# Recurrence bounds in the first three steps, and the output gate's SiLU as one pass of ScalarE, in a hybrid attention and recurrence block

## The chip, the cores and the metric

The kernel runs on one core of a Trainium2 chip. The core has five engines, each with its own instruction queue that runs in order: TensorE (PE, matrix products into PSUM banks), VectorE (DVE), ScalarE (ACT, which applies functions from a loaded table), GpSimd (POOL) and SyncE (SP). SP, ACT and POOL can issue DMA transfers; in this kernel SP issues nearly all of them. The engines meet only through semaphores. The metric is the device time of one execution in microseconds (us); the median of several runs is compared.

## The reference

One layer of a trunk with 256 tokens and a width of 2048, in float32. The parts that matter here:

```python
a = rmsnorm(h, norm_mix_pre[layer])
proj = a @ w_in[layer]
q_a, k_a, v_a, q_r, f_r, i_r, g_r, gate_a, gate_r = split_columns(proj)
...
lower_bounds = jnp.cumsum(jax.nn.softmax(hgrn_lower_bounds, axis=0), axis=0)
lb = lower_bounds[layer].reshape(HGRN_HEADS, HGRN_KEY_DIM)[None, :, None, :]
q_h = jax.nn.silu(rheads(q_r))
f = lb + (1.0 - lb) * jax.nn.sigmoid(rheads(f_r))
r_out = hgrn2_chunked(q_h, jnp.log(f), 1.0 - f, rheads(i_r))
...
r_out = r_out * lax.rsqrt(jnp.mean(r_out * r_out, axis=-1, keepdims=True) + NORM_EPS)
r_out = r_out * hgrn_norm_gain[layer]
r_out = r_out.reshape(B, S, HGRN_HEADS * HGRN_VAL_DIM) * jax.nn.silu(g_r)
y = jax.nn.sigmoid(gate_a) * (attn @ w_attn_branch) + jax.nn.sigmoid(gate_r) * (r_out @ w_hgrn_branch)
h = h + rmsnorm(y @ w_mix_out, norm_mix_post)
```

A SwiGLU feed-forward layer with its own norms follows. The change touches two small things: how the 1024 lower bounds `lb` of the recurrence are made, and how the output gate, SiLU of `g_r` times the gain of the recurrence's norm, is made.

## The kernel before

**Products.** Every float32 weight tile is split into a high part (ACT rounds it) and a low part (DVE subtracts), and each product takes three matmuls: high by high, high by low, low by high. PE then runs an almost unbroken stream of matmuls. A *wide block* is 1024 columns of the projection, worked in 8 *steps* of 256 rows of depth. One step loads 1 MB of weights into one of three `raw` buffers (SP, lines 244 to 260), is split two steps ahead of its use (`split_wide`, line 333; a buffer is loaded again once its split is over), and is multiplied in `multiply_wide` (line 365).

**Plain steps and seven-product steps.** A plain step has 24 matmuls; its split is one pass of ACT (L342) and one of DVE (L344). For some pairs of rows a Strassen-like scheme with 21 matmuls is used: its split needs sums on DVE (L348, L354, L355), three passes of ACT (L353, L356, L359) and two more of DVE (L360 for `wl`, L362 for `dl`), and it uses sums of the activations, which `pair_sums` (line 449) makes once, for three pairs (0, 1 and 2), in four pieces each: f (L454), s (L434 to L438), a high part on ACT (L440) and a low part on DVE (L441).

**The first blocks.** Block 0 is the output gate `g_r` (steps 0 to 7, all plain). Block 1 is the first half of the branch gate `gate_a` (steps 8 to 15; steps 10, 12 and 14 have seven products), block 2 is its second half (steps 16 to 23; the same pattern), block 3 is the first half of `gate_r`. Block 0 adds into the four `acc` banks of PSUM; the others use `acc` and `aux` banks in turn.

**What sets the order.** The program order of each queue is fixed by the main loop (line 1394 on). In each step it first prepares (splits the tiles of two steps later, loads further ones), multiplies, advances the evacuations of finished blocks (`evacs`), and advances two *lanes*. A lane is a queue of generators, of which the first is advanced by one `yield`. In a wide block the lanes advance twice per step: once between the halves of the step's matmuls (line 286) and once at its end (line 1420). In block 0 the preparation, too, stands between the halves, behind the transposes of the next part of x (`more_x`, line 670).

Lane 0 holds `opening` (line 606) from the start:
- advances 1 to 8: squares of x on ACT (L596);
- advance 9 (middle of step 4): four DMAs on SP (gain row, feed-forward norm gain, lower bounds, rope table; L609 to L614), then the norm's factor `r1c` (`rsqrt_mean`, line 120: ACT Ln and Exp, a few tiny DVE operations) and the diagonal matrices for `row_broadcast` (line 542);
- advance 12: a matmul that spreads the factor; advance 13: ACT copies it to `rowb`;
- advance 14 (end of step 6): PE transposes 32 rows of `rowg` (L622);
- advance 15: DVE copies the columns to `colg` (L624), and takes maximum and differences (L627 to L629); ACT two Exp (L630, L631);
- advance 16: four tiny DVE operations give `lb` and `lb1` (L633 to L636);
- 24 empty advances, then at advances 40 to 43 the four rope tables on DVE (L641), and at 44 two mask loads on SP (L645, L646).

Lane 1 gets `pair_sums` in the middle of step 2 (advance 5), so its twelve pieces run at advances 5 to 16.

**The gate.** When step 7 is over, `evac_g` (line 749) takes block 0 out of the `acc` banks, two of its four keys at the end of step 7 and two at the end of step 8. Per key: ACT writes the sigmoid of the scaled bank into `sig` (L755), DVE multiplies the scaled bank with it (L756, which reads the bank a second time), and DVE multiplies with the gain row (L759). Block 1 needs the `acc` banks again from step 10 on. `stored` (line 728) evacuates blocks 1 to 3: DVE adds (L719), ACT's Sigmoid (L734), and a DMA from ACT's queue to memory (L737).

**Tables.** ACT's functions come from table sets, and the profile shows each exchange as an ACT_TABLE_LOAD on ACT. Line 152 asks for the set with Ln and Exp at the start. Elsewhere the program either asks ahead (`preload_act_table_set`), or a load is put directly ahead of the instruction that needs it when the kernel is built, as at L755.

Of the kernel before, what the change touches and what calls it, by code (L numbers as in the profile page):

```python
# [17 lines left out]
AF = mybir.ActivationFunctionType  # L18
OP = mybir.AluOpType

P = 128
# [59 lines left out]
def tile_hybrid_block(ctx: ExitStack, tc: tile.TileContext, t, out):  # L81
    nc = tc.nc
# [12 lines left out]
    def nm(s):  # L95
        serial[0] += 1
        return f"{s}_{serial[0]}"
# [7 lines left out]
    def aux():  # L105
        return auxp.tile([P, 512], F32, tag="aux", name=nm("aux"))
# [7 lines left out]
    def small(s, n=8, bufs=6):  # L114
        return cpool.tile([P, n], F32, tag=f"small{n}", bufs=bufs, name=nm(s))

    def mm(ps, lhsT, rhs, start, stop):
        nc.tensor.matmul(ps, lhsT, rhs, start=start, stop=stop, skip_group_check=True)  # L118

    def rsqrt_mean(dst, ss, n, bias=None):  # L120

        w = ss.shape[-1]
        v, y, a = (small(s)[:, :w] for s in ("v", "y", "a"))
        bias = bias or (eps[:, 0:1], eps[:, 1:2])
        nc.scalar.activation(y, ss, AF.Ln, scale=1.0 / n, bias=bias[0])
        nc.scalar.activation(y, y, AF.Exp, scale=-0.5)
        nc.vector.tensor_scalar(v, ss, -0.5 / n, bias[1], op0=OP.mult, op1=OP.add)  # L130
        if w == 1:
            nc.vector.scalar_tensor_tensor(out=a, in0=y, scalar=v, in1=y, op0=OP.mult, op1=OP.mult)
        else:
            nc.vector.tensor_mul(a, y, y)
            nc.vector.tensor_mul(a, a, v)
        nc.vector.scalar_tensor_tensor(
            out=dst, in0=a, scalar=1.5, in1=y, op0=OP.add, op1=OP.mult
        )
# [6 lines left out]
    ident = cpool.tile([P, P], F32, name="ident")  # L145
# [3 lines left out]
    nc.gpsimd.memset(eps[:, 1:2], -0.5 * EPS)  # L149
    rowg = cpool.tile([48, P], F32, name="rowg")  # L150
    nc.scalar.dma_start(rowg[0:16], t["norm_mix_pre"][0].rearrange("(a p) -> a p", p=P))
    nc.scalar.preload_act_table_set("natural_log_exp_and_others")
    colg = cpool.tile([P, 48], F32, name="colg")
    r1c = cpool.tile([P, 2], F32, name="r1c")
# [13 lines left out]
    lb = kp.tile([P, 120], F32, name="lb")[:, :8]  # L168
    lb1 = kp.tile([P, 8], F32, name="lb1")
# [4 lines left out]
    gainr = wide_pool[0].tile([P, HW], F32, name="gainr")  # L174
# [5 lines left out]
    def ptile(s):  # L180
        pool, n = (wide_pool[-1], 2) if wide_pool else (fp[0], 5)
        return pool.tile([P, 512], F32, tag="p", bufs=n, name=nm(s))
# [281 lines left out]
    class Split:  # L464
# [20 lines left out]
        def high(self, n, src):  # L485
            nc.scalar.activation(self.slots[n][:, :, 0, :], src, AF.Copy)

        def low(self, n, src):
            x = self.slots[n]
            nc.vector.tensor_sub(x[:, :, 1, :], src, x[:, :, 0, :].bitcast(F32))  # L490
            self.there.add(n)
# [22 lines left out]
    def transpose_in(src, gcol, dst, c, apart=False):  # L514

        ps = []
        for k in (2 * c, 2 * c + 1):
            if apart or not ps:
                bank = aux()
            ps.append(bank[:, :S] if apart else bank[:, (k % 2) * S : (k % 2 + 1) * S])  # L520
            for b in range(2):
                nc.tensor.transpose(  # L522
                    ps[-1][:, b * P : (b + 1) * P],
                    src[k // 4][:, b, (k % 4) * P : (k % 4 + 1) * P],
                    ident,
                )
        def high(kk):
            k = 2 * c + kk
            nc.scalar.activation(dst(k)[0], ps[kk], AF.Copy, scale=gcol[:, k : k + 1])  # L529

        def low(kk):
            k = 2 * c + kk
            nc.vector.scalar_tensor_tensor(
                out=dst(k)[1], in0=ps[kk], scalar=gcol[:, k : k + 1],
                in1=dst.f32(k), op0=OP.mult, op1=OP.subtract,
            )

        if apart:
            return high, low
        high(0), high(1), low(0), low(1)  # L540

    def row_broadcast(dst, rc):

        ds = [small("diag", P, 2) for _ in range(2)]
        for b in range(2):
            nc.vector.tensor_scalar(ds[b], ident, rc[:, b : b + 1], None, op0=OP.mult)
        yield
        yield
        yield
        ps = aux()  # L550
        for b in range(2):
            mm(ps[:, b * P : (b + 1) * P], ones[:, :P], ds[b], True, True)
        yield
        nc.scalar.activation(dst, ps[:, :S], AF.Copy)
# [4 lines left out]
    evacs, turns, lanes, queue = deque(), deque(), [deque(), deque()], deque()  # L559
    ready = set()  # L560
# [31 lines left out]
    def sumsq(dst, pieces):  # L592
        for j, x in enumerate(pieces):
            for b in range(2):
                junk = ptile("junk")
                nc.scalar.activation(  # L596
                    junk, x[:, b, :], AF.Square, accum_out=dst[:, 4 * b + j : 4 * b + j + 1]
                )
                yield

    def add_parts(dst, ss):
        nc.vector.tensor_reduce(
            dst, ss.rearrange("p (b j) -> p b j", b=2), op=OP.add, axis=mybir.AxisListType.X
        )

    def opening():
        ss, s2 = small("ss"), small("s2")
        yield from sumsq(ss, xt)
        nc.sync.dma_start(gainr, t["hgrn_norm_gain"].to_broadcast([P, HW]))  # L609
        nc.sync.dma_start(rowg[0:16], t["norm_ffn_pre"][0].rearrange("(a p) -> a p", p=P))  # L610
        nc.sync.dma_start(
            rowg[16:32], t["hgrn_lower_bounds"].rearrange("l (a p) -> (l a) p", p=P)
        )
        nc.sync.dma_start(cs, t["rope"])  # L614
        add_parts(s2[:, :2], ss)
        rsqrt_mean(r1c, s2[:, :2], D)
        ready.add("r1c")
        yield from row_broadcast(rowb, r1c)
        ready.add("rowb")
        yield  # L620
        ps = aux()
        nc.tensor.transpose(ps[:, :32], rowg[:32], ident[:32, :32])  # L622
        yield
        nc.vector.tensor_copy(colg[:, 16:48], ps[:, :32])  # L624
        l0, l1 = colg[:, 32:40], colg[:, 40:48]
        m, e0, e1 = small("m"), small("e0"), small("e1")
        nc.vector.tensor_max(m, l0, l1)  # L627
        nc.vector.tensor_sub(e0, l0, m)
        nc.vector.tensor_sub(e1, l1, m)  # L629
        nc.scalar.activation(e0, e0, AF.Exp)  # L630
        nc.scalar.activation(e1, e1, AF.Exp)  # L631
        yield
        nc.vector.tensor_add(e1, e0, e1)  # L633
        nc.vector.reciprocal(e1, e1)
        nc.vector.tensor_mul(lb, e0, e1)
        nc.vector.tensor_scalar(lb1, lb, -1.0, 1.0, op0=OP.mult, op1=OP.add)  # L636
        ready.add("lb")
        for _ in range(24):
            yield
        for i, (j, c) in enumerate(((0, -QSCALE), (1, -QSCALE), (0, 1.0), (1, 1.0))):  # L640
            nc.vector.scalar_tensor_tensor(  # L641
                out=tabs[:, i, :], in0=cs[:, j, :], scalar=c, in1=rowb, op0=OP.mult, op1=OP.mult
            )
            yield
        nc.sync.dma_start(amask, t["amask"])  # L645
        nc.sync.dma_start(lmask, t["lmask"])  # L646

    def keep_warm(n):

        ps = aux()  # L650
        for _ in range(n):
            mm(ps, warm[:, :P], warm, True, True)

    def start():
        keep_warm(WARM)
        ps = aux()
        nc.tensor.transpose(ps[:, :16], rowg[:16], ident[:16, :16])
        nc.vector.tensor_copy(colg[:, :16], ps[:, :16])
        high, low = transpose_in(xt, colg, xT, 0, True)
        for kk in range(2):  # L660
            high(kk)
            low(kk)
            split_first(0, kk)
        keep_warm(BRIDGE)
        transpose_in(xt, colg, xT, 1)
        split_first(0, 2)
        split_first(0, 3)
        lanes[0].append(opening())

    def more_x(c):  # L670
        if 0 < c < KD // 2 - 1:
# [5 lines left out]
    fT, qT, gN, iN = {}, {}, {}, {}  # L677
# [71 lines left out]
    def evac_g(b):  # L749
        def then(key, src):  # L750
            s, g = key
            if s == 0:
                gN[g] = hslot("g")
            sig = ptile("sig")
            nc.scalar.activation(sig, src, AF.Sigmoid, scale=r1c[:, s : s + 1])  # L755
            nc.vector.scalar_tensor_tensor(  # L756
                out=sig, in0=src, scalar=r1c[:, s : s + 1], in1=sig, op0=OP.mult, op1=OP.mult
            )
            nc.vector.tensor_mul(gN[g][:, s, :], sig, gainr[:, g * 512 : (g + 1) * 512])  # L759
        return totals(b, then)  # L760

    def nslot(s):
# [631 lines left out]
    for i in range(len(items)):  # L1394
        kind, n, _ = items[i]
# [92 lines left out]
```

## Time and profile before

| | |
|---|---|
| Median of three runs | 1722.13 us (1721.88 to 1722.79) |
| Profiled execution | 1722.56 us |
| Span of the profiled execution | 1720.8 us |
| Granted clock of TensorE | 0.998 |
| Steps 0 to 7 on PE (block 0) | 8.15 to 55.56 us |
| Steps 8 to 15 (block 1) | 55.56 to 102.61 us |
| DMA packets | 207189, 338.48 MB |

How to read what follows: a timeline row has the start in us, the duration (of all instructions merged into it), the engine (a "q" behind it is its queue's own work, as issuing a DMA), the source line, the operation, the tiles out<-in with their sizes, and the count. What stands in brackets is the idle time of the engine before it and what ended that: "[1.05 <-DVE dl L362]" means that the engine stood 1.05 us and went on when DVE had written `dl` in line 362. A group row has the line, engine, operation and tiles, the count, the durations (lowest, median and highest ns), and first and last start. A DMA row has the tiles, the queue, the count, the size and the median us from issue to landing. Matmul ends are modelled, since matmuls are pipelined; starts are the better measure, and a wait of PE seen by its starts is a little longer than the bracket says.

### The profile page before, as it was taken

Reading aid. Unit: us, or ns where it says so; the run is one execution under the profiler, and the core shown is the slowest. Engines: PE = TensorE matmul, PEld = TensorE weight load, DVE = VectorE, ACT = ScalarE, POOL = GpSimd, SP = SyncE. Lnnn points to the kernel's source line nnn. Section 1 sums busy time; section 2 is a strip of 40 time slices with the busy share of each in tenths; the row PEclk is TensorE's granted clock in tenths of the full one; section 3 lists DMA queues with packets and bytes.
Section 4 is the critical chain, followed back from the end, with each engine's and each line's share of the span. In section 5 each row is a group of like instructions: output and inputs, shape, how many; then the busy total and the mean of one; then the engine's idle time right before and its main releaser. Section 6 shows DMA issues by size and latency. Waiting matters only on the chain.

```text
span 1720.8 us, 21495 instructions
## 1 busy us (share of the span) xinstructions
PE 1703.5 (99%) x8356; PEld 1429.9 (83%) x8357; DVE 1358.7 (79%) x1486; ACT 898.7 (52%) x1016; POOL 6.5 (0%) x16
## 2 busy tenths in 40 slices
PE   9999999999999999999999999999999999999997
PEld 7788888888888888888888878888888888888886
DVE  6888888866787877774566578888888888898997
ACT  6455555544434434445444466555555555665663
POOL 0000000000000000000000000000000000000000
PEclk9999999999999999999999999999999999999999
DMA  8466666655544545475456745555556555656663
GB/s 289 162 237 241 232 221 220 229 189 194 172 159 160 197 135 163 155 254 187 159 172 204 245 163 196 196 197 200 201 202 202 201 202 197 221 191 215 201 197 114
DMA packets 207189, 338.48 MB, mean 197 GB/s; under 512 B 10688, under 2 KB 77424, under 8 KB 207088
## 3 DMA queue, kind: packets, MB, share of 16 engines
q1 hardware_dynamic: 201360, 325.71, 56.9%
q10 hardware_dynamic: 5728, 11.41, 1.8%
q8 instruction: 65, 1.06, 0.3%
q14 instruction: 36, 0.29, 0.1%
HBM read 328.69 MB, written 8.39 MB: 196 GB/s over the span
## 4 chain that ended last, share of the span: by engine, by line
PE 89%; DVE 6%; issue 2%; ACT 2%; DMA 1%; ACTq 0%; DVEq 0%; SPq 0%
PE acc L118 61%; PE aux L118 26%; DVE wl L344 1%; DVE wl L360 1%; DVE dl L362 1%; DVE sum L348 1%; ACT w L356 1%; ACT w L342 0%; PE aux L522 0%; DVE sum L355 0%; DVE sum L354 0%; PE aux L840 0%; DMA gpost<-in_norm_mix_post 0%; DMA raw<-in_w_ffn_gate_up 0%; PE aux L1166 0%
## 5 line engine op out<-in xcount | busy, mean ns | idle before, releaser
L297 DVE TENSOR_TENSOR w<-raw,w 128x1024 fp32r<-128x1024 f32 x224 | 274.1, 1224 | 194.9 <-ACT w L296 193.1
L296 ACT ACTIVATE w<-raw 128x1024 fp32r<-128x1024 f32 x224 | 237.0, 1058 | 292.8 <-PE acc L118 263.0
L118 PE MATMUL acc<-xT,w 128*128 128x256 f32 (+1 forms) x2048 | 366.6, 338 | 0.0
L118 PEld LDWEIGHTS acc<-xT,w 128*128 128x128 f32 x2048 | 311.6, 188 | 44.0
L344 DVE TENSOR_TENSOR wl<-raw,w 128x2048 fp32r<-128x2048 f32 (+1 forms) x131 | 284.1, 2173 | 48.7 <-ACT w L342 46.4
L342 ACT ACTIVATE w<-raw 128x2048 fp32r<-128x2048 f32 (+1 forms) x131 | 237.7, 1819 | 103.1 <-PE acc L118 34.9
L360 DVE TENSOR_TENSOR wl<-sum,w 128x2048 fp32r<-128x2048 f32 x63 | 144.3, 2291 | 57.4 <-ACT w L356 57.4
L118 PE MATMUL acc<-w,hT 128*128 128x512 f32 x622 | 183.1, 391 | 0.3 <-ACT hT L529 0.3
L118 PE MATMUL acc<-w,xT 128*128 128x512 f32 x578 | 169.4, 392 | 0.0
L353 ACT ACTIVATE w<-sum 128x1024 fp32r<-128x1024 f32 x63 | 67.0, 1063 | 195.6 <-DVE sum L348 195.6
L118 PE MATMUL aux<-w,hT 128*128 128x512 f32 x430 | 137.3, 389 | 0.0
L118 PEld LDWEIGHTS acc<-w,hT 128*128 128x128 f32 x622 | 116.1, 188 | 24.5 <-ACT hT L529 0.5
L118 PEld LDWEIGHTS acc<-w,xT 128*128 128x128 f32 x578 | 108.1, 188 | 22.2
L362 DVE TENSOR_TENSOR dl<-raw,dh 128x1536 fp32r<-128x1536 f32 x63 | 110.4, 1752 | 0.0
L118 PE MATMUL aux<-w,xT 128*128 128x512 f32 x344 | 109.8, 389 | 0.0
L359 ACT ACTIVATE dh<-raw 128x1536 fp32r<-128x1536 f32 x63 | 93.2, 1479 | 6.6 <-PE aux L118 3.4
L118 PEld LDWEIGHTS aux<-w,hT 128*128 128x128 f32 x430 | 80.7, 188 | 16.8
L118 PE MATMUL acc<-w,yT 128*128 128x512 f32 x384 | 88.2, 390 | 0.1
L118 PEld LDWEIGHTS acc<-w,yT 128*128 128x128 f32 x384 | 71.8, 188 | 15.3 <-DVE w L297 0.5
L118 PE MATMUL acc<-w,a 128*128 128x512 f32 x268 | 83.7, 389 | 0.5 <-DVE e L1200 0.5
L118 PE MATMUL aux<-w,a 128*128 128x512 f32 x268 | 83.7, 389 | 0.0
L118 PE MATMUL aux<-wl,hT 128*128 128x512 f32 x215 | 83.6, 389 | 0.0
(262 smaller groups left out, 2624.2 us busy)
## 6 DMA issues: line engine op xcount, KB each, us to landing
raw<-in_w_in SPq DMA_DIRECT2D x270, 512.0 KB, 4.6
raw<-in_w_ffn_gate_up SPq DMA_DIRECT2D x176, 512.0 KB, 4.6
raw<-in_w_ffn_down SPq DMA_DIRECT2D x88, 512.0 KB, 4.8
raw<-in_w_mix_out SPq DMA_DIRECT2D x32, 512.0 KB, 4.9
raw<-in_w_hgrn_branch SPq DMA_DIRECT2D x16, 512.0 KB, 4.6
raw<-in_w_attn_branch SPq DMA_DIRECT2D x16, 512.0 KB, 4.5
waits<-e ACTq DMA_DIRECT2D x24, 256.0 KB, 2.6
v<-waits SPq DMA_DIRECT2D x6, 512.0 KB, 7.0
```

The lines of the kernel that those rows point to most:

```text
L118: nc.tensor.matmul(ps, lhsT, rhs, start=start, stop=stop, skip_group_check=True)
L296: nc.scalar.activation(wh, raw, AF.Copy)
L297: nc.vector.tensor_sub(wl, raw, wh.bitcast(F32))
L342: nc.scalar.activation(hi[:, c], raw[:, c], AF.Copy)
L344: nc.vector.tensor_sub(lo[:, c], raw[:, c], hi[:, c].bitcast(F32))
L348: nc.vector.tensor_sub(s[:, :1024].rearrange("p (a c) -> p a c", a=2), raw[:, 512:1536].rearrange("p (a c) -> p a c", a=2), raw[:, None, : ...
L353: nc.scalar.activation(hi[:, :1024], s[:, :1024], AF.Copy)
L356: nc.scalar.activation(hi[:, 1024:], s[:, 1024:], AF.Copy)
L359: nc.scalar.activation(dhi, d, AF.Copy)
L360: nc.vector.tensor_sub(lo, s, hi.bitcast(F32))
L362: nc.vector.tensor_sub(dlo, d, dhi.bitcast(F32))
```

## The change

The two small loads of `rowg` (feed-forward norm gain and lower bounds) leave `opening`, where SP issued them at advance 9, and are issued by POOL at the start, into rows of their own. The bounds' transpose, copy and arithmetic become a generator of their own, `bounds`, which is put on lane 1 at the start: two empty advances, then its four pieces at advances 3 to 6. `pair_sums` comes into lane 1 behind it. `opening` loses three pieces' work and two of its advances, so the 24 empty advances, the rope tables and the mask loads come two advances earlier. Behind the norm's Ln and Exp, `opening` asks for the table set with Silu. `evac_g` writes Silu of the scaled bank straight into the gate's tile on ACT, and DVE does one product with the gain row.

```diff
@@ -149,6 +149,10 @@
     rowg = cpool.tile([48, P], F32, name="rowg")
     nc.scalar.dma_start(rowg[0:16], t["norm_mix_pre"][0].rearrange("(a p) -> a p", p=P))
+    nc.gpsimd.dma_start(rowg[16:32], t["norm_ffn_pre"][0].rearrange("(a p) -> a p", p=P))
+    nc.gpsimd.dma_start(
+        rowg[32:48], t["hgrn_lower_bounds"].rearrange("l (a p) -> (l a) p", p=P)
+    )
     nc.scalar.preload_act_table_set("natural_log_exp_and_others")
@@ -607,26 +611,38 @@
         nc.sync.dma_start(gainr, t["hgrn_norm_gain"].to_broadcast([P, HW]))
-        nc.sync.dma_start(rowg[0:16], t["norm_ffn_pre"][0].rearrange("(a p) -> a p", p=P))
-        nc.sync.dma_start(
-            rowg[16:32], t["hgrn_lower_bounds"].rearrange("l (a p) -> (l a) p", p=P)
-        )
         nc.sync.dma_start(cs, t["rope"])
         add_parts(s2[:, :2], ss)
         rsqrt_mean(r1c, s2[:, :2], D)
         ready.add("r1c")
+        nc.scalar.preload_act_table_set("silu_and_others")
         yield from row_broadcast(rowb, r1c)
         ready.add("rowb")
         yield
+        for _ in range(24):
+            yield
+        for i, (j, c) in enumerate(((0, -QSCALE), (1, -QSCALE), (0, 1.0), (1, 1.0))):
...
+        nc.sync.dma_start(amask, t["amask"])
+        nc.sync.dma_start(lmask, t["lmask"])
+
+    def bounds():
+
+        for _ in range(2):
+            yield
         ps = aux()
-        nc.tensor.transpose(ps[:, :32], rowg[:32], ident[:32, :32])
-        yield
-        nc.vector.tensor_copy(colg[:, 16:48], ps[:, :32])
+        nc.tensor.transpose(ps[:, :48], rowg, ident[:48, :48])
+        yield
+        nc.vector.tensor_copy(colg[:, 16:48], ps[:, 16:48])
...
         nc.vector.tensor_sub(e1, l1, m)
+        yield
         nc.scalar.activation(e0, e0, AF.Exp)
         nc.scalar.activation(e1, e1, AF.Exp)
         yield
@@ -635,15 +651,6 @@
         ready.add("lb")
-        for _ in range(24):
-            yield
-        for i, (j, c) in enumerate(((0, -QSCALE), (1, -QSCALE), (0, 1.0), (1, 1.0))):
...
-        nc.sync.dma_start(amask, t["amask"])
-        nc.sync.dma_start(lmask, t["lmask"])
@@ -666,6 +673,7 @@
         lanes[0].append(opening())
+        lanes[1].append(bounds())
@@ -751,12 +759,9 @@
-            sig = ptile("sig")
-            nc.scalar.activation(sig, src, AF.Sigmoid, scale=r1c[:, s : s + 1])
-            nc.vector.scalar_tensor_tensor(
-                out=sig, in0=src, scalar=r1c[:, s : s + 1], in1=sig, op0=OP.mult, op1=OP.mult
-            )
-            nc.vector.tensor_mul(gN[g][:, s, :], sig, gainr[:, g * 512 : (g + 1) * 512])
+            d = gN[g][:, s, :]
+            nc.scalar.activation(d, src, AF.Silu, scale=r1c[:, s : s + 1])
+            nc.vector.tensor_mul(d, d, gainr[:, g * 512 : (g + 1) * 512])
```

More of the change, by code (lines that the diff above doesn't have):

```diff
@@ L620, in opening @@
         yield
-        ps = aux()
-        nc.tensor.transpose(ps[:, :32], rowg[:32], ident[:32, :32])
-        yield
[L624 to L631, printed above, removed]
-        yield
[L633 to L637, printed above, removed]
         for _ in range(24):
@@ L646, in opening @@
         nc.sync.dma_start(lmask, t["lmask"])
+    def bounds():
+        for _ in range(2):
+            yield
+        ps = aux()
+        nc.tensor.transpose(ps[:, :48], rowg, ident[:48, :48])
+        yield
+        nc.vector.tensor_copy(colg[:, 16:48], ps[:, 16:48])
+        l0, l1 = colg[:, 32:40], colg[:, 40:48]
+        m, e0, e1 = small("m"), small("e0"), small("e1")
+        nc.vector.tensor_max(m, l0, l1)
+        nc.vector.tensor_sub(e0, l0, m)
+        nc.vector.tensor_sub(e1, l1, m)
+        yield
+        nc.scalar.activation(e0, e0, AF.Exp)
+        nc.scalar.activation(e1, e1, AF.Exp)
+        yield
+        nc.vector.tensor_add(e1, e0, e1)
+        nc.vector.reciprocal(e1, e1)
+        nc.vector.tensor_mul(lb, e0, e1)
+        nc.vector.tensor_scalar(lb1, lb, -1.0, 1.0, op0=OP.mult, op1=OP.add)
+        ready.add("lb")
     def keep_warm(n):
```

## The prediction

> **What bounds the kernel now.** I began with the page: which engine fills the span.
>
> ```profile
> span 1720.8 us, 21495 instructions
> PE 1703.5 (99%) x8356; PEld 1429.9 (83%) x8357; DVE 1358.7 (79%) x1486; ACT 898.7 (52%) x1016; POOL 6.5 (0%) x16
> ```
>
> PE is busy all but 17.3 us. The change adds and removes almost no PE work, so it can only win back time in which PE stands still, or lose more of it. Next came the stretches around the change, and who made PE wait over the whole run (in the windows: start:end, length, then busy time and instructions of PE, PEld, DVE, ACT and POOL, clock, DMA share, GB/s; in the waits: total, times, longest).
>
> ```profile
> 8.00:47.50 39.50, 39.50 (x191) 32.78 (x190) 28.81 (x48) 26.58 (x49) 0.00 (x0) 1.00 0.84 298
> 55.50:92.50 37.00, 32.91 (x141) 25.62 (x140) 31.69 (x36) 21.30 (x21) 0.00 (x0) 1.00 0.45 154
> ```
>
> ```profile
> PE acc L118 <- DVE wl L360: 1.7, 2, 1.5
> PE aux L118 <- DVE dl L362: 1.5, 2, 1.1
> ...
> PE acc L118 <- DVE sig L756: 0.9, 1, 0.9
> ```
>
> Up to 47.5 PE never rests. Between 55.5 and 92.5 it loses 4.1 of 37 us, with the clock at 1.00, waiting for VectorE (DVE): for the split weights (L360, L362), and once for the gate itself (L756). The PE timeline shows what the stretch would take without waits.
>
> ```profile
> 55.56 0.39 PE L118 MATMUL aux<-w,xT 128*128 128x512 f32 x1
> ...
> 85.62 0.39 PE L118 MATMUL aux<-w,xT 128*128 128x512 f32 x1
> ...
> 91.06 0.39 PE L118 MATMUL aux<-dh,xT 128*128 128x512 f32 x1
> 92.50 0.50 PE L118 MATMUL aux<-dl,xT 128*128 128x512 f32 x1 [1.05 <-DVE dl L362]
> ```
>
> The step from 85.62 to 91.06 has 24 matmuls, one every 0.227 us. Steps 8 to 13 have 24, 24, 21, 24, 21 and 24, and step 14 one before it needs dl: 139 in all, 31.5 us. So the matmul of 92.50 could start at 87.1. **At most 5.4 us are to be had.**
>
> **What DVE does in that stretch.** Its timeline decides how much of the 5.4 comes back.
>
> ```profile
> 52.02 0.68 DVE L454 TENSOR_TENSOR f<-xT 128x512 f32<-128x512 f32 x1
> ...
> 53.68 2.29 DVE L344 TENSOR_TENSOR wl<-raw,w 128x2048 fp32r<-128x2048 f32 x1
> 55.88 0.18 DVE L624 COPY colg<-aux 128x32 f32<-128x32 f32 x1
> ...
> 57.56 0.68 DVE L441 TENSOR_TENSOR so<-s,so 128x512 fp32r<-128x512 f32 x1
> 59.37 0.75 DVE L756 SCALAR_TENSOR_TENSOR sig<-acc,r1c,sig 128x512 f32<-128x512 f32 x1 [1.12 <-ACT sig L755]
> ...
> 61.54 0.69 DVE L759 TENSOR_TENSOR g<-sig,gainr 128x512 f32<-128x512 f32 x1
> 62.15 1.22 DVE L348 TENSOR_TENSOR sum<-raw 128x1024 f32<-128x1024 f32 x1
> ...
> 69.83 0.75 DVE L756 SCALAR_TENSOR_TENSOR sig<-acc,r1c,sig 128x512 f32<-128x512 f32 x1
> ...
> 72.61 2.28 DVE L344 TENSOR_TENSOR wl<-raw,w 128x2048 fp32r<-128x2048 f32 x1
> ...
> 90.69 1.75 DVE L362 TENSOR_TENSOR dl<-raw,dh 128x1536 fp32r<-128x1536 f32 x1
> ```
>
> ```profile
> 57.35 1.28 ACT L755 ACT_TABLE_LOAD   x1
> 58.64 1.27 ACT L755 ACTIVATE sig<-acc,r1c 128x512 f32<-128x512 f32 x2
> ```
>
> From 52.02 on DVE works or waits for ScalarE (ACT). From 55.88 to 57.56 stand the bounds; at 59.37 it waits 1.12 us for a sigmoid that stood behind a 1.28 us table load; then come two pairs of gate instructions, and only at 62.15 the sums that PE wants at step 10. The second two pairs run from 69.83 to 72.61. One DVE instruction starts about 0.08 before the last has ended (61.54 plus 0.69 is 62.23, the next starts at 62.15).
>
> **The new order, step by step.** Bounds leave this stretch. But they now lead lane 1 for six advances, so the pair sums behind them run two advances (one step) later. At 52.02 DVE now does the low part of pair 1 (0.68 less 0.08: 0.60) instead of f and s of pair 2 (53.68 less 52.02: 1.66); the split of step 9 runs from 52.62 to 54.82 (55.88 less 53.68: 2.20); f and s of pair 2 take until 56.48; two products (0.61 each) until 57.70. Silu delays none of this: its first two banks are full half way through step 7 (12 matmuls before 55.56: 52.8), ACT's copy for step 9 has to be over by 52.6 for DVE's split in any case, and its table is loaded. The sum L348 so starts at 57.70 instead of 62.15: **4.45 won.** From there to the next gate nothing changes (69.83 less 62.15: 7.68). Of the 2.78 us up to 72.61 there remain two products and the low part of pair 2: 1.82, **0.96 won.** Together 5.41; L362 ends 5.41 sooner and PE gets dl at 87.1, just as it arrives. Two limits nearly agree: 5.4.
>
> One activation each is a fair swap:
>
> ```profile
> 68.33 1.91 ACT L342 ACTIVATE w<-raw 128x2048 fp32r<-128x2048 f32 x1
> ```
>
> ```profile
> L1184 ACT ACTIVATE g<-acc,r2c x2: 679/684/688, 1036.0 to 1038.0; 128x512 f32<-128x512 f32 x2
> ```
>
> A Silu of this shape takes 684 ns; two sigmoids at 58.64 took 1.27. The accumulator banks are let go by ACT alone, before 64, so the wait on L756 goes. ACT's copy for step 11, at 68.33 before, moves up 4.45 with the sums and back 0.6 for pair 2's high part, now ahead of it: it ends at 66.4, and DVE wants it at 67.2, a margin of 0.8.
>
> **What moves into the opening.** I cost it at nothing: PE's transpose is moved, not added, and DVE is idle 10.7 of 39.5 us there. The cover is thinnest at step 5, where the Silu load now stands behind the norm, ahead of pair 0's high part and the activations of xT:
>
> ```profile
> 39.50 0.20 ACT L129 ACTIVATE y<-y 128x2 f32<-128x2 f32 x1
> ...
> 40.72 0.84 ACT L529 ACTIVATE xT<-aux,colg 128x256 fp32r<-128x256 f32 x2 [1.02 <-PE aux L522]
> ...
> 42.38 0.87 DVE L533 SCALAR_TENSOR_TENSOR xT<-aux,colg,xT 128x256 fp32r<-128x256 f32 x2
> ...
> 43.66 0.48 PE L118 MATMUL acc<-w,xT 128*128 128x512 f32 x1
> ```
>
> ACT has the norm's Exp done at 39.7; load and high part take it to 41.6, and xT's activations run 0.9 later. DVE, freed of f and s here, does one low part after 41.6 and L533 again at 42.3. Unchanged, with 0.4 us to spare (42.38 plus 0.87 is 43.25, due at 43.66).
>
> The two small loads leave SP's queue, behind which the rope and weight loads stand; those wait for DVE to free a buffer, so nothing is won. On POOL nothing is queued behind them until the recurrence. No POOL transfer is in this trace; the nearest rows:
>
> ```profile
> rowg<-in_norm_mix_pre ACTq DMA_DIRECT2D x1, 8.0 KB, 3.0
> ...
> rowg<-in_hgrn_lower_bounds SPq DMA_DIRECT2D x1, 8.0 KB, 5.8
> ```
>
> ```profile
> 16.42 0.60 PE L522 MATMUL aux<-ident,x 128*128 128x128 f32 x4
> ```
>
> From issue to landing they took 3.0 and 5.8. PE's FIFO reaches the moved transpose behind those of 16.42, at about 17 us: to be late the two would have to be issued at 11, and only a few memsets stand ahead of them on POOL. Nothing.
>
> **What the change gives back.** Block 1's gates still use Sigmoid (L734), and now Silu's table is the one loaded. Before, L755 had loaded Sigmoid's. No row shows Sigmoid behind Silu, so the price lies between 0 and one load, 1.28. I take the load, as one stood at 57.35 where Exp gave way to Sigmoid. It falls here, and the four rope tables (L641) come one step earlier:
>
> ```profile
> 109.46 0.71 ACT L734 ACTIVATE e<-e,r1c 128x512 f32<-128x512 f32 x1
> ...
> 113.75 2.29 DVE L344 TENSOR_TENSOR wl<-raw,w 128x2048 fp32r<-128x2048 f32 x1 [1.57 <-ACT w L342]
> ```
>
> ```profile
> 132.18 1.75 DVE L362 TENSOR_TENSOR dl<-raw,dh 128x1536 fp32r<-128x1536 f32 x1
> 133.85 0.76 DVE L641 SCALAR_TENSOR_TENSOR tabs<-cs,rowb 128x256 f32<-128x256 f32 x2
> ```
>
> ```profile
> 140.42 0.69 DVE L424 TENSOR_TENSOR e<-aux,e 128x512 f32<-128x512 f32 x1 [0.48 <-PE acc L118]
> ```
>
> ```profile
> 134.12 0.40 PE L118 MATMUL acc<-dl,xT 128*128 128x512 f32 x1
> ...
> 175.41 0.39 PE L118 MATMUL aux<-dh,xT 128*128 128x512 f32 x1
> ...
> 176.23 0.50 PE L118 MATMUL aux<-dl,xT 128*128 128x512 f32 x1 [0.43 <-DVE dl L362]
> ```
>
> Queued behind those sigmoids on ACT is the copy that DVE already awaits at 113.75, so DVE runs 1.28 plus 0.09 (a lost overlap) late. Two of the tables move from behind L362 to ahead of it: 0.76 less 0.08 more. At 132.18 DVE is 2.05 late, its dl ends at 133.93, and PE used it at 134.12 with 0.13 to spare: **PE loses 1.92.** At 176.23 PE waited 0.59 for the next dl (175.64 was its due time). DVE is only about 1 us late by then, because the tables are then done in both kernels and the wait of 0.48 at 140.42 shrinks; so those 0.59 come back: 1.33 lost. If the wait at 140.42 is truly PE's, it travels with PE, and 1.92 stays lost.
>
> The Trainium skill ("ScalarE: Activation LUTs", Table sets: the hidden batching unit) gives each set one expensive function and lists sigmoid as the anchor of a set of its own, and advises batching calls by set. That speaks against this change; by it the load at L734 is certain, without it the sum would be the first rival's. No run here shows it yet.
>
> **Sum.** 5.4 less 1.33 is 4.1, less 1.92 is 3.5; I take 3.9, nearer the first. The profiled execution took 1722.56 (1.8 around its span), 0.43 above the median of the three runs, and would go to 1718.7; from the median of 1722.13 it is **1718.2**.
>
> **Rivals.** (1) Silu's set holds Sigmoid, no second load: only the tables' 0.68 less 0.13 is lost: 5.4 less 0.55, 1717.3. (2) The exchange costs two loads' time, 2.56: DVE 3.3 late, PE loses 3.2 and gets 0.59 back, 2.8 won, 1719.3. For it: nothing in the rows, a sigmoid starts 0.01 behind the load at 57.35. The same page (What ACT_TABLE_LOAD costs) adds a drain of about 1.38 us to the 1.28, 2.66 together, nearly this case; the row at 58.64 shows no such gap behind the load. (3) Another order on ACT eats the win: in the opening the whole load, 1.28 less 0.4, reaches PE, or the 0.8 margin at step 11 fails by as much; 0.9 to 2 us less, 1719.1 to 1720.2. (4) The change does not do what it says: the bounds' time (55.88 to 57.56) and the wait at 59.37 don't come back, because the later pair sums and Silu's own wait fill them: 5.4 less 2.8 less the 1.9 given back, 0.7 won, 1721.4. (5) Slower: the POOL transfers land late and hold PE's FIFO at the transpose in step 1, one for one. It decides from a landing at 17 us, eats the win at 21 and is slower by 0.2% at 24.3; at 26 it gives 1727. The 8 KB rows (3.0 and 5.8) speak against it.
>
> **How the numbers follow.** Forecast 0.52 (1717.6 to 1718.8), rivals 0.08, 0.10, 0.15, 0.08, 0.07. 0.2%, about what a measurement of this kernel can tell, is 3.4 us: faster means under 1718.7. That is most of the forecast and rival 1: 0.55; the forecast's edge, rivals 2, 3 and 4 are the same: 0.38; rival 5 slower: 0.07. The range goes from 5.4 won with nothing lost (1716.7) to the far end of rival 3 (1720.5), leaving out rivals 4 and 5.
>
> **What would show it.** PE without waits from 55.6 to about 87; L348 at 57.7 behind two products; one table load after the norm near 39.7 and one ahead of L734 near 104; a new PE wait on dl near 131 of 1.5 to 2 us. Wrong if PE waits before 47, if L734 has no load, or if ACT delays DVE at step 11.

## The result, and the profile after

The changed kernel takes 1718.28 us (median of 12 runs, 1717.84 to 1719.16) against 1722.47 us for the kernel before (12 runs): 4.2 us less, a ratio of 0.9976 with a 95% interval of 0.9967 to 0.9985. The profiled execution took 1718.07 us. Lines of the changed kernel's code have other numbers: L344 is now L348, L348 is L352, L360 is L364, L362 is L366, L342 is L346, L441 is L445, L440 is L444, L438 is L442, L454 is L458, L424 is L428, L734 is L742, L641 is L625; the gate's activation is L763 and its product L764. In some of the experiments a line moves by one or two more.

First the head of the page and the waits of PE over the whole run:

```profile
span 1716.2 us, 21493 instructions
...
PE 1701.7 (99%) x8357; PEld 1430.4 (83%) x8357; DVE 1356.1 (79%) x1482; ACT 900.0 (52%) x1017; POOL 7.6 (0%) x18
```

```profile
PE acc L118 <- DVE dl L366: 1.5, 1, 1.5
...
PE aux L118 <- DVE dl L366: 0.2, 1, 0.2
```

The waits on `wl` and on the gate are gone. One wait on `dl` is nearly gone (0.2), and a new one of 1.5 has come. The DVE timeline of the stretch that lost time before:

```profile
52.03 0.69 DVE L445 TENSOR_TENSOR so<-s,so 128x512 fp32r<-128x512 f32 x1
52.63 2.29 DVE L348 TENSOR_TENSOR wl<-raw,w 128x2048 fp32r<-128x2048 f32 x1
54.83 0.69 DVE L458 TENSOR_TENSOR f<-xT 128x512 f32<-128x512 f32 x1
...
56.49 1.29 DVE L764 TENSOR_TENSOR g<-g,gainr 128x512 f32<-128x512 f32 x2
57.70 1.22 DVE L352 TENSOR_TENSOR sum<-raw 128x1024 f32<-128x1024 f32 x1
...
65.37 1.29 DVE L764 TENSOR_TENSOR g<-g,gainr 128x512 f32<-128x512 f32 x2
...
67.17 2.29 DVE L348 TENSOR_TENSOR wl<-raw,w 128x2048 fp32r<-128x2048 f32 x1
...
85.26 1.75 DVE L366 TENSOR_TENSOR dl<-raw,dh 128x1536 fp32r<-128x1536 f32 x1
```

DVE starts the sums at 57.70 (62.15 before) and step 11's split at 67.17 (72.61 before), with no wait for the gate in between. PE, in the same stretch and two blocks on:

```profile
55.15 0.39 PE L118 MATMUL aux<-w,xT 128*128 128x512 f32 x1
...
87.06 0.50 PE L118 MATMUL aux<-dl,xT 128*128 128x512 f32 x1 [0.25 <-DVE dl L366]
...
128.46 0.39 PE L118 MATMUL acc<-dh,xT 128*128 128x512 f32 x1
130.39 0.50 PE L118 MATMUL acc<-dl,xT 128*128 128x512 f32 x1 [1.54 <-DVE dl L366]
...
172.04 0.39 PE L118 MATMUL aux<-dl,xT 128*128 128x512 f32 x1
```

From the first matmul of step 8 to the `dl` of step 14 PE needs 31.91 us (87.06 less 55.15) instead of 36.94 (92.50 less 55.56). At step 22 it then waits 1.54 for `dl`, which it hardly did before; at step 30 (172.04) it waits no more. What lies behind the wait of step 22 stands on ACT and DVE:

```profile
39.72 1.28 ACT L618 ACT_TABLE_LOAD   x1
...
52.26 1.27 ACT L763 ACTIVATE g<-acc,r1c 128x512 f32<-128x512 f32 x2
...
103.88 1.28 ACT L742 ACT_TABLE_LOAD   x1
105.17 0.72 ACT L742 ACTIVATE e<-e,r1c 128x512 f32<-128x512 f32 x1
```

```profile
109.48 2.29 DVE L348 TENSOR_TENSOR wl<-raw,w 128x2048 fp32r<-128x2048 f32 x1 [3.01 <-ACT w L346]
...
119.37 0.42 DVE L625 SCALAR_TENSOR_TENSOR tabs<-cs,rowb 128x256 f32<-128x256 f32 x1
...
121.91 0.75 DVE L625 SCALAR_TENSOR_TENSOR tabs<-cs,rowb 128x256 f32<-128x256 f32 x2
...
128.58 1.75 DVE L366 TENSOR_TENSOR dl<-raw,dh 128x1536 fp32r<-128x1536 f32 x1
```

The second load stands ahead of the branch gate's first sigmoid, and DVE's wait for the copy behind it is 3.01 instead of 1.57; three of the four tables now stand ahead of step 22's `dl` instead of one.

The opening started at its own time in each profile (the first matmul of block 0 came between 7.23 and 8.99 us in the thirteen profiles of this study, whatever the edit). So the experiments are compared by two things: the medians beside the kernel before, and three stretches of PE's timeline, which an early or late opening doesn't move. Each difference is taken to the median of the kernel before that was run beside it (1721.88 to 1722.47). The difference in time and the one in the sum of the stretches disagree by up to 1.0 us, and the changed kernel, run twice, won 4.19 and 3.05. So for less than about 1 us the stretches decide, and even they differ by 0.3 between the two profiles of the changed kernel.

| Kernel | Time less that of the kernel before (us) | Step 8 to dl of step 14 | to dl of step 22 | to dl of step 30 | Sum of the three |
|---|---|---|---|---|---|
| before | | 36.94 | 41.62 | 42.11 | 120.67 |
| changed | -4.19 | 31.91 | 43.33 | 41.65 | 116.89 |
| changed, again | -3.05 | 31.91 | 43.66 | 41.62 | 117.19 |
| bounds only, scratch tiles | +1.88 | 38.98 | 42.07 | 41.64 | 122.69 |
| bounds only, in place | -1.87 | 35.05 | 42.14 | 41.61 | 118.80 |
| Silu only | -2.37 | 33.79 | 42.83 | 41.86 | 118.48 |
| changed, Silu through scratch | +0.74 | 35.16 | 43.60 | 41.62 | 120.38 |
| changed, no early Silu load | -2.96 | 31.90 | 43.44 | 41.65 | 116.99 |
| changed, rowg loads on ACT | -4.15 | 31.92 | 43.58 | 41.65 | 117.15 |
| changed, Silu in branch gates | -4.91 | 31.90 | 42.07 | 41.65 | 115.62 |
| changed, tables back | -4.05 | 31.90 | 42.88 | 41.85 | 116.63 |
| changed, Sigmoid asked for early | -4.37 | 31.91 | 42.12 | 41.61 | 115.64 |
| the same, and tables back | -4.93 | 31.91 | 41.63 | 41.60 | 115.14 |

### The profile page after: what moved, and what is told of

The parts are those of the page before. It is cut to its first block, busy times and chain, and to the rows that moved or that the text cites. A ratio compares the mean times of both kernels' runs of the same rounds, so it can differ in the third digit from the quotient of the medians.

```text
span 1716.2 us, 21493 instructions
## 1 busy us (share of the span) xinstructions
PE 1701.7 (99%) x8357; PEld 1430.4 (83%) x8357; DVE 1356.1 (79%) x1482; ACT 900.0 (52%) x1017; POOL 7.6 (0%) x18
## 4 chain that ended last, share of the span: by engine, by line
PE 89%; DVE 6%; issue 2%; ACT 2%; DMA 0%; ACTq 0%; DVEq 0%
PE acc L118 60%; PE aux L118 27%; DVE wl L348 2%; DVE wl L364 1%; DVE sum L352 1%; DVE dl L366 1%; ACT w L360 1%; ACT w L346 0%; PE aux L526 0%; DVE sum L358 0%; DVE sum L359 0%; PE aux L845 0%; DMA gpost<-in_norm_mix_post 0%; PE aux L1171 0%; DVE fz L1301 0%
## 5 line engine op out<-in xcount | busy, mean ns | idle before, releaser
L348 DVE TENSOR_TENSOR wl<-raw,w 128x2048 fp32r<-128x2048 f32 (+1 forms) x131 | 284.3, 2174 | 50.4 <-ACT w L346 48.0
L346 ACT ACTIVATE w<-raw 128x2048 fp32r<-128x2048 f32 (+1 forms) x131 | 237.8, 1819 | 102.6 <-PE acc L118 36.1
L364 DVE TENSOR_TENSOR wl<-sum,w 128x2048 fp32r<-128x2048 f32 x63 | 144.4, 2291 | 57.5 <-ACT w L360 57.5
L366 DVE TENSOR_TENSOR dl<-raw,dh 128x1536 fp32r<-128x1536 f32 x63 | 110.4, 1752 | 0.0
L118 PE MATMUL acc<-wl,hT 128*128 128x512 f32 x215 | 83.6, 389 | 0.0
```

Of the source, the lines that this page charges most:

```text
L346: nc.scalar.activation(hi[:, c], raw[:, c], AF.Copy)
L348: nc.vector.tensor_sub(lo[:, c], raw[:, c], hi[:, c].bitcast(F32))
L364: nc.vector.tensor_sub(lo, s, hi.bitcast(F32))
L366: nc.vector.tensor_sub(dlo, d, dhi.bitcast(F32))
```

## The experiments: what made the win

**The bounds alone.** The changed kernel with the old gate, and without the early request for Silu's table:

```diff
-        nc.scalar.preload_act_table_set("silu_and_others")
...
-            d = gN[g][:, s, :]
-            nc.scalar.activation(d, src, AF.Silu, scale=r1c[:, s : s + 1])
-            nc.vector.tensor_mul(d, d, gainr[:, g * 512 : (g + 1) * 512])
+            sig = ptile("sig")
+            nc.scalar.activation(sig, src, AF.Sigmoid, scale=r1c[:, s : s + 1])
+            nc.vector.scalar_tensor_tensor(
+                out=sig, in0=src, scalar=r1c[:, s : s + 1], in1=sig, op0=OP.mult, op1=OP.mult
+            )
+            nc.vector.tensor_mul(gN[g][:, s, :], sig, gainr[:, g * 512 : (g + 1) * 512])
```

> Bounds moved, pair sums later, rope tables one step earlier, as in the changed kernel; the gate as before (sigmoid and two VectorE operations per key). Theory (bounds and gate each take their own VectorE time out of the stretch): from 52.03 VectorE runs 0.60, 2.20 and 1.66 to 56.49, then two pairs of gate operations, 2.78, so L352 starts at 59.3 (62.15 before, 57.70 with the whole change); the split of step 11 starts at 70.3 (72.61 before), and PE's dl of step 14 at 90.2 (92.50): 2.3 won. No table load at the branch gate's sigmoid, so only the tables (0.7) press at step 22: a PE wait of 0.3 to 0.6 there, won back at step 30. Time 2.3 us under before: 1720.2. Rival (the bounds alone carry the win, the gate's second pass was hidden): 1718.3. Rival (the gate alone carries it): 1722.4.

Measured: 1724.03 us against 1722.15, a ratio of 1.0012 (1.0003 to 1.0021). Neither the theory (1720.2) nor a rival (1718.3, 1722.4) had it that slow. The ACT and DVE timelines of this run:

```profile
56.68 1.28 ACT L762 ACT_TABLE_LOAD   x1 [4.26 <-DVE s L442]
57.97 0.69 ACT L762 ACTIVATE sig<-acc,r1c 128x512 f32<-128x512 f32 x1
60.27 0.69 ACT L762 ACTIVATE sig<-acc,r1c 128x512 f32<-128x512 f32 x1 [1.60 <-DVE g L766]
```

```profile
58.70 0.75 DVE L763 SCALAR_TENSOR_TENSOR sig<-acc,r1c,sig 128x512 f32<-128x512 f32 x1 [2.10 <-ACT sig L762]
...
60.99 0.75 DVE L763 SCALAR_TENSOR_TENSOR sig<-acc,r1c,sig 128x512 f32<-128x512 f32 x1 [0.81 <-ACT sig L762]
...
62.38 1.22 DVE L352 TENSOR_TENSOR sum<-raw 128x1024 f32<-128x1024 f32 x1
```

DVE does come to the gate early, as forecast, but ACT has not begun: its first sigmoid waits 4.26 us until DVE has made `s` of pair 2 (L442), and its second until DVE has written the first `g` (L766). `sig`, `f` and `s` all come from `ptile`, which has two tiles at this time. Before the change the high part of pair 2 stood ahead of the gate on ACT:

```profile
56.72 0.61 ACT L440 ACTIVATE so<-s 128x512 fp32r<-128x512 f32 x1
```

With the pair sums one step later, `s` holds one tile across the first half of the gate, the sigmoids take turns on the other, and no key overlaps the next. A new theory: the scratch tiles, not the arithmetic. The next run keeps the old arithmetic and takes the scratch tile away.

**The bounds alone, gate in place.** The changed kernel, without the early request for Silu's table, and with both passes of the old gate in the gate's own tile:

```diff
-        nc.scalar.preload_act_table_set("silu_and_others")
...
             d = gN[g][:, s, :]
-            nc.scalar.activation(d, src, AF.Silu, scale=r1c[:, s : s + 1])
+            nc.scalar.activation(d, src, AF.Sigmoid, scale=r1c[:, s : s + 1])
+            nc.vector.scalar_tensor_tensor(
+                out=d, in0=src, scalar=r1c[:, s : s + 1], in1=d, op0=OP.mult, op1=OP.mult
+            )
             nc.vector.tensor_mul(d, d, gainr[:, g * 512 : (g + 1) * 512])
```

> The bounds alone again, but the sigmoid is written into the gate's own tile, not into one of the two scratch tiles that the pair sums also use. Theory (moving the pair sums later made the gate wait for scratch: s of pair 2 holds one of the two tiles, and the gate's keys take turns on the other): ScalarE loads its table and does both sigmoids before 56, VectorE runs without waits from 52.0, L352 starts at 59.3 as first forecast (62.4 in the run with scratch tiles), the split of step 11 at 70.3 (74.3), the dl of step 14 35 us after step 8's first matmul (36.9 before). Time 2 to 2.5 us under the kernel before, 1719.9. Rival (bounds moved without the Silu lose by themselves, because pair sums fall into the stretch): 1724, as with scratch tiles.

Measured: 1720.01 against 1721.88, a ratio of 0.9988 (0.9979 to 0.9997), and 35.05 us to the dl of step 14. The DVE timeline of this run has the gate without a wait:

```profile
55.97 0.74 DVE L763 SCALAR_TENSOR_TENSOR g<-acc,r1c,g 128x512 f32<-128x512 f32 x1
...
58.74 1.22 DVE L352 TENSOR_TENSOR sum<-raw 128x1024 f32<-128x1024 f32 x1
```

The sums come 2.77 behind the first gate operation, 58.74 in a profile in which step 8 began 0.5 sooner than in the changed kernel's. The first forecast for the bounds holds once no scratch tile is shared: 1.9 won instead of 1.9 lost.

**Silu through a scratch tile.** The whole change, but with the tile put back:

```diff
             d = gN[g][:, s, :]
-            nc.scalar.activation(d, src, AF.Silu, scale=r1c[:, s : s + 1])
-            nc.vector.tensor_mul(d, d, gainr[:, g * 512 : (g + 1) * 512])
+            sig = ptile("sig")
+            nc.scalar.activation(sig, src, AF.Silu, scale=r1c[:, s : s + 1])
+            nc.vector.tensor_mul(d, sig, gainr[:, g * 512 : (g + 1) * 512])
```

> The changed kernel, with Silu written into a scratch tile instead of the gate's tile. Theory (the two scratch tiles bind the bounds' move and the gate together): the first Silu waits until s of pair 2 is over at 56.5, the second until the first product is; L352 starts at 59.3 instead of 57.7, the split of step 11 at about 70.2 instead of 67.2, and of the 5.0 won up to step 14 about 2.5 are left. Time 2 to 3 us over the changed kernel: 1720.8. Rival (scratch tiles don't matter with only one VectorE operation per key): 1718.3.

Measured: 1722.74 against 1722.00, a ratio of 1.0005 (0.9996 to 1.0013): no win is left that the medians could show, and 0.3 us of it in the three stretches. Its ACT timeline shows the same chain as the bounds alone:

```profile
56.99 0.69 ACT L764 ACTIVATE sig<-acc,r1c 128x512 f32<-128x512 f32 x1 [4.28 <-DVE s L442]
58.50 0.69 ACT L764 ACTIVATE sig<-acc,r1c 128x512 f32<-128x512 f32 x1 [0.82 <-DVE g L765]
```

The stretch to step 14 costs 35.16, 3.25 more than with Silu in place, where about 2.5 was expected. The time is 4.5 us over the changed kernel's (3.9 over its repeat), where 2 to 3 was. The direction was right, the size too small: counted from step 8's first matmul, DVE starts the split of step 11 3.24 later than in the changed kernel, with a wait of 0.51 for ACT's copy just ahead of it. Writing the gate in place is worth about as much in this stretch as the single pass is: with the old two passes in place it took 35.05, 3.14 more than with Silu in place.

**Silu alone.** The kernel before, with the three lines of the new gate in `evac_g` and nothing else.

> The gate's SiLU in one pass, nothing else; bounds and tables where they were, and the Silu table loaded just ahead of the gate. Theory: the load stays on the chain at 57.35, the first product starts at 59.4 and the sums L348 at 60.6 (62.15 before): 1.55 won, and 1.56 more at the second pair; PE's dl of step 14 at 89.4, 3.1 won. Then Sigmoid has to be loaded ahead of the branch gate's sigmoid, VectorE falls 1.2 to 1.4 back there, PE waits 1.0 to 1.3 at step 22 and gets 0.6 back at step 30. Time 2.4 us under before, 1720.0. Rival (the gate alone carries the whole win): 1718.3. Rival (it wins nothing without the bounds): 1722.4.

Measured: 1719.78 against 1722.15, 0.9987 (0.9978 to 0.9995). The stretch to step 14 takes 33.79, 3.15 less than before (3.1 expected), and step 22 gives 1.2 back. With the tile in place the two halves of the change add up: 1.89 for the bounds and 3.15 for Silu make 5.04, and the whole change won 5.03. Here the pair sums are not delayed, so two scratch tiles might have done; that was not run.

**No early load of Silu's table.**

```diff
-        nc.scalar.preload_act_table_set("silu_and_others")
```

> The changed kernel without the request for the Silu table behind the norm: the load then stands directly ahead of the gate's first Silu. Theory (moving bounds and pair sums has already taken ScalarE off the chain there): load at 52.3 to 53.6, both Silus over by 55, before VectorE wants them at 56.5; L352 still at 57.7 and no change of time: 1718.3. Rival (the early load is a third of the win): L352 1.3 later, 1719.5.

Measured: 1719.04 against 1722.00 (0.9983, 0.9975 to 0.9992), and 31.90 us to step 14. The ACT timeline of this run:

```profile
51.90 1.28 ACT L762 ACT_TABLE_LOAD   x1
53.19 1.27 ACT L762 ACTIVATE g<-acc,r1c 128x512 f32<-128x512 f32 x2
```

Both Silus are over at 54.5, DVE's first product is due at 55.98 in this profile. In the changed kernel the early load is worth nothing in the stretches: ACT has room there once the bounds' Exp have left. The median doesn't decide between the theory and the rival: it lies 2.96 under the kernel before, the changed kernel's two lie 4.19 and 3.05 under it.

**The two rowg loads on ACT's queue** instead of POOL's (`nc.scalar.dma_start` in both lines).

> The changed kernel with the two loads of rowg issued by ScalarE at the start instead of POOL. Theory (their queue doesn't matter, they land at 6 us and are used at 16.6): no change, 1718.3; the first matmul between 7.2 and 8.2 as in the other profiles. Rival (POOL's transfers, or the instructions that make their descriptors, delay the opening): 0.5 us less.

Measured: 1717.85 against 1722.00 (0.9978, 0.9969 to 0.9987), first matmul at 7.66, and the three stretches as in the two profiles of the changed kernel. It wins 4.15 beside the kernel before, the changed kernel 4.19 and 3.05. POOL costs nothing that can be seen; a cost below 0.5 us in the opening can't be told apart from the opening's own spread.

## The experiments: what is given back

**The changed kernel again**, beside the same runs of the kernel before as the last two experiments of this section and as the bounds in place:

> The changed kernel once more, on the same chip and beside the same runs of the kernel before as the next three. Expected 4.2 us under the kernel before, and from the first matmul of step 8 to the dl of step 14 31.9 us (36.9 before).

Measured: 1718.83 against 1721.88 (0.9983, 0.9974 to 0.9992). It won 3.05 us instead of the expected 4.2. The stretch to step 14 is 31.91 to the hundredth; the wait at step 22 is 0.35 longer than in the first profile, and the opening of this one began latest of all.

**Silu in the branch gates**, so that no exchange is needed there:

```diff
-            (k0, k1), AF.Copy if k0[0] == "v" else AF.Sigmoid
+            (k0, k1), AF.Copy if k0[0] == "v" else AF.Silu
```

> The changed kernel with Silu in place of Sigmoid in the branch gates of blocks 1 to 3 (their values are then others), so that no table is exchanged at the branch gate; the exchange comes later, at the forget gate. Theory (the reload pays most of what is given back): PE gets dl of step 14 at 87.1 as in the changed kernel; the wait of VectorE for the copy of step 19 falls from 3.0 to about 1.6, PE's wait at step 22 from 1.5 to 0.5 or less (the tables are left), and step 30 takes that back. Time 1.2 us under the changed kernel, 1717.1. Rival (the reload is hidden, the tables and the mask loads cost it): wait at step 22 still 1.5, 1718.3.

Measured: 1717.24 against 1722.15 (0.9972, 0.9961 to 0.9982). The stretch from step 14 to step 22 takes 42.07 instead of 43.33, and PE's wait at step 22 is small:

```profile
128.89 0.50 PE L118 MATMUL acc<-dl,xT 128*128 128x512 f32 x1 [0.29 <-DVE dl L366]
```

That is 1.3 us for a load of 1.28.

**The tables back** behind 26 empty advances instead of 24:

> The changed kernel with 26 empty advances in place of 24, so that the four rope tables and the mask loads stand where they stood before. Theory (tables 0.7 of the 1.7 that PE loses at step 22): dl of step 14 unchanged at 87.1, PE's wait at step 22 falls from 1.5 to 0.9, net 0.6 to 0.8 us less: 1717.6. Rival (the reload alone sets that wait): 1718.3, wait unchanged.

Measured: 1718.10 against 1722.15 (0.9978, 0.9968 to 0.9987). The wait at step 22 falls only from 1.54 to 1.08, and 0.2 of that returns at step 30 (41.85 instead of 41.65), where DVE sets the pace again. The direction was right, the size of 0.6 to 0.8 is not shown: in the sum of the stretches it is 0.26 against the first profile of the changed kernel and 0.56 against its repeat, and the medians can't tell.

**Sigmoid asked for early**, where ACT is idle:

```diff
-        return totals(b, then)
+        def go():
+            yield from totals(b, then)
+            yield
+            nc.scalar.preload_act_table_set("sigmoid_and_others")
+
+        return go()
```

> The changed kernel, with the Sigmoid table asked for at the end of step 9, behind the last Silu and behind ScalarE's copy for step 11, where ScalarE is idle for 4 us. Theory (the reload costs because it stands between dh and the copy that VectorE waits for, not by its length): VectorE's wait for the copy of step 19 is 1.6 instead of 3.0, PE's wait at step 22 0.3 instead of 1.5, as in the run with Silu in the branch gates, but with the reference's values. Time 0.7 to 1.2 us under the changed kernel: 1717.2. Rival (any exchange there costs 1.3 us, wherever it stands): no change.

Measured: 1717.51 against 1721.88 (0.9973, 0.9963 to 0.9984), beside 1718.83 for the changed kernel: all of its seven runs are below all eleven of that one. The load and the wait that it no longer makes, on ACT and DVE:

```profile
64.68 1.92 ACT L346 ACTIVATE w<-raw 128x2048 fp32r<-128x2048 f32 x1
66.62 1.28 ACT L769 ACT_TABLE_LOAD   x1
71.00 1.06 ACT L357 ACTIVATE w<-sum 128x1024 fp32r<-128x1024 f32 x1 [3.09 <-DVE sum L352]
```

```profile
108.55 2.29 DVE L348 TENSOR_TENSOR wl<-raw,w 128x2048 fp32r<-128x2048 f32 x1 [1.58 <-ACT w L346]
```

The same 1.28 us load now stands in a gap of ACT, which still waits 3.09 for DVE behind it, and DVE's wait is back at 1.58. The place of the load cost 1.3 us, not the load.

**The same, and the tables back:**

> The same, and the rope tables where they stood before (26 empty advances). Theory: no wait of PE at step 22; at step 30 a wait like the 0.6 of the kernel before comes back, as VectorE sets that one. Against the run without this: 0 to 0.3 us less, 1717.1. Rival (the tables cost their whole 0.7): 1716.5.

Measured: 1716.95 against 1721.88, a ratio of 0.9971 (0.9959 to 0.9982), the fastest kernel of this study: 4.9 us under the kernel before and 1.9 under the changed one beside it. In PE's waits nothing is left between steps 8 and 30 but the 0.24 at step 14. The tables are worth 0.5 in the stretches. The wait that was expected to return at step 30 did not: from step 22 on it takes 41.60.

## Why the prediction was right

- **The stretch of steps 8 to 14.** 5.4 was forecast, and `dl` came at 87.06 (87.1 forecast, 92.50 before). That the clock times agree so closely is luck: the first matmul of block 0 came 0.38 earlier in this profile (7.77 against 8.15), and step 8's 0.41 earlier. The stretch itself gained 5.03, and PE's wait for that `dl` was then 0.25. The order on DVE was as worked out, with the sums at 57.70 and step 11's split at 67.17 (67.2).
- **The opening at nothing.** The load stands at 39.72, step 6 is on time, POOL is of no account. But "PE's transpose is moved, not added" leaves out what stands behind it, and that term is 0.41, not nothing. Before, the bounds' transpose came behind the last transposes of x; in the changed kernel it stands ahead of the last five of them (before, then after):

```profile
46.50 0.60 PE L522 MATMUL aux<-ident,x 128*128 128x128 f32 x4
...
49.77 0.24 PE L622 MATMUL aux<-ident,rowg 32*128 32x32 f32 x1
```

```profile
16.58 0.26 PE L637 MATMUL aux<-ident,rowg 48*128 48x48 f32 x1
...
46.50 0.60 PE L526 MATMUL aux<-ident,x 128*128 128x128 f32 x4
```

  From the first matmul of block 0 to the transposes of 46.50 it is now 38.73 us instead of 38.35, and from there to step 8's first matmul 8.65 instead of 9.06. PE loses nothing by that. But ACT's `xT` and copy, and DVE's split behind them, wait for these transposes, so DVE comes into the stretch later with respect to PE: it starts the split of step 8 5.33 to 5.34 us ahead of step 8's first matmul in all eleven profiles with the bounds moved, and 5.75 in the two without. These 0.41 us are what lies between 5.44 and 5.03, and between the 2.3 forecast for the bounds alone and the 1.89 measured in place.
- **One activation each is a fair swap.** True, but the sum was right in part by luck. It took the product's early start from ACT being free and the table being loaded. What it needs as well, and doesn't name, is that Silu asks for no scratch tile; with one, 3.25 us of the stretch are gone, and the bounds without the new gate lose time. And "its table is loaded" was no condition at all: without the early load nothing changes.
- **The load ahead of Sigmoid.** Forecast at L734 near 104, it stands at 103.88. PE was to lose 1.92 at step 22 and lost 1.70 (`dh` to `dl` 1.93 instead of 0.23; 2.05 in the repeat). The run with Silu in the branch gates and the one with Sigmoid asked for early show that the load makes 1.2 to 1.3 of it. The tables cost DVE what was put in the sum: from the split at 109.48 to `dl` at 128.58 it takes 19.10 us, and 18.43 both before and with the tables back. What was put too high is DVE's lateness ahead of them: 1.37 in the sum, 1.17 in the trace (the split starts 22.42 us behind the `dl` of step 14, 21.25 before). Before, DVE had waited 0.18 at 99.82 for a copy whose raw tile was late, and in this profile it doesn't. In the repeat it waits 0.25 there and is 1.51 late.
- **What comes back at step 30.** 0.59 forecast, 0.46 seen (42.11 less 41.65). The number speaks for the 4.1 and against the 3.5 of the prediction's two sums, but its mechanism, that the loss of step 22 itself comes back in part, is not shown: the run with Sigmoid early and the tables back loses nothing at step 22 and takes 41.60 all the same. DVE's wait of 0.48 at 140.42 stands in the profile of the kernel before alone; in the changed kernel L428 follows L427 by 0.79 without a wait, and so in every other run. Why the kernel before has it stays open.
- **Sum.** 3.9 forecast against 4.2 by the medians (3.1 in the repeat), 3.8 and 3.5 in the stretches of the two profiles. The terms were 5.4, 1.92 and 0.59 against 5.03, 1.70 and 0.46, so part of its closeness is that the errors go against each other.
- **The rivals.** (1) fell with the load at 103.88. (2) fell with its price: 1.28, and the next function 0.01 behind it. The Trainium skill ("ScalarE: Activation LUTs", What ACT_TABLE_LOAD costs) adds a drain of about 1.38 us. Here the load at 103.88 follows the end of dh by some hundredths and the one at 66.62 follows a copy that ended at 66.60. The trace disagrees with that addition. (3) and (5) show nowhere: at step 11 ACT's copy ends at 66.31, and DVE wants it at 67.17. (4) names what did not happen, but the two scratch-tile runs are of its kind: DVE waiting for the activation took the win.

## What to carry to other kernels

When work is moved in a hand-written order, count the scratch tiles as well as the engines: a generator that runs one step later holds its tile one step later, and a pool of two tiles then couples things that share no data. A function of another table set brings a load (1.28 us here), which costs time if something waits behind it, so ask for the set in a gap of ScalarE's queue that the profile shows, also for the set that comes next. And an edit that wins at the first stall can lose at the next one that the same engine sets, so follow its lateness to the next step where it is due. Compare lengths of stretches and not clock times of two profiles: an opening that came 0.4 us sooner hid a cost of the same size here.

## What the hardware showed that was not expected

No pause stands around a table load in these traces: it took 1.28 us in each of the four cases shown (39.72, 51.90, 66.62, 103.88) and began some hundredths of a us behind the activation ahead. Where the next activation had nothing else to wait for, it began 0.01 behind the load. The first matmul of block 0 came between 7.23 and 8.99 us in thirteen profiles, with no pattern by edit. In the latest one PE stood 1.78 for the transfer of x just before; why that transfer takes longer in one profile than in another stays open. The spread alone is enough to hide a difference of 1 us between two single executions.
